# Fourth block's product added last, behind the next chunk's first three; down units at three places a chunk; forms made earlier

## The chip, the cores and the metric

One core of a Trainium2 chip runs the whole kernel in one launch. The metric is the device time of one execution in microseconds (us), the median of several runs; smaller is better. Engines are named as the profile names them: PE (TensorE matmuls), PEld (TensorE weight loads, which overlap PE), DVE (VectorE), ACT (ScalarE), POOL (GpSimd), SP (SyncE, which issues most transfers). L12 is line 12 of the kernel's file.

## The reference, cut to what matters

Two layers of an encoder trunk, for one sequence of 512 tokens and 1024 features, in float32:

```python
# a layer
h = rms_norm(x, attn_norm)
...                               # three branches: latent attention, grouped attention, pooling
x = x + merged @ w_out            # 1024 -> 1024, "out-projection"
# the feed-forward part (FFN)
h = rms_norm(x, ffn_norm)
ud = depthwise_conv(h @ w_up, w_conv, b_conv)    # 1024 -> 2 * 2816, conv of width 3 over tokens
gate, val = split(ud)
x = x + (silu(gate) * val) @ w_down              # 2816 -> 1024
```

The change touches the FFN, and the end of the out-projection where the FFN's inputs are made.

## The kernel before

**Layout.** Activations lie with features on the 128 partitions and the 512 tokens along the free axis. The residual is `XM`, eight rows (m = 0 to 7) of 128 features by 512 tokens. PE multiplies in a reduced float type, so every operand is held as two halves, high and low, whose sum is the float32 value; a product is three matmuls (high x high, high x low, low x high; `mm3`, L526). `HH` and `HL` are the halves of the scaled residual, `wh` and `wl` those of a weight, `ah` and `al` those of an activation. A low half is high subtracted from the value: on VectorE, on POOL, or "by transfer" (L438), where ScalarE writes the negated high half and a transfer that POOL issues adds the value onto it. All V., A. and G. calls pass through one-line wrappers, so the profile gives them few lines: L299 activation, L306 tensor_tensor, L310 scalar_tensor_tensor, L314 reduction, L318 tensor_scalar, L322 copy.

**The FFN's up-projection.** It has 22 chunks of 128 gate and 128 value features each. Chunks 0 to 3 are computed plainly: two units of 24 matmuls of 128x512 each (`plain`, tokens "u"). Chunks 4 to 21 are computed as 2x2 block products (gate and value by left and right halves of the features, against left and right 256 tokens), with seven products instead of eight (tokens "f", function `product`). Each product has a name, "11", "12", "1", "22", "2", "4", "3", and is twelve matmuls of 128x256, four for each pair of input rows q = 0 to 3 with three matmuls each. It needs one form of the weights (made by `w_form` from the chunk's four weight tiles a11, a12, a21, a22) and one form of the input (made once a layer by `build_forms(q)`). Forms 11, 12 and 22 of the weights are plain halves in tiles `fh` and `fl`, by transfer; forms 1, 2, 4 and 3 are sums or differences on VectorE (`total`), then halves in `wh` and `wl`.

For a chunk, 11 goes to PSUM bank acc; 2 and then 3 are added onto it. 1 goes to bank AV, and 4 is added onto it. 12 and 22 go to banks of their own with tag ST. Between them ScalarE copies intermediate values out to `sx` (keys s1, s5, s2, s4), and VectorE adds them into `u` (gate) and `v` (value): with product 3 done, VectorE does v[hi] = acc + s5, then v[lo] = acc + s4, where s4 is the copy of 22. Scaling, convolution, silu and the product of gate and value follow.

**The FFN's down-projection.** Tokens "d" are units of three matmuls of 128x512, for one output row m and one chunk. `_groups()` splits the 22 chunks in groups of 4, 5, 5, 5, 3; the units of a group become possible behind its last chunk, and are dealt over the chunks of the next group, at four places of a chunk: behind products 22, 2, 4 and 3 (SPOTS). Six units are kept for the end (KEEP times 3), and the last group's units stand behind the last chunk. Units of one m add up in one bank, tag mi or S in turn.

**What sets the order.** `_ffn()` writes a list of tokens, and PE follows it. The other engines' work is issued by a planner with costs in us (`chain`, whose argument `after` is how many us of planned PE time a chain waits before its steps are issued; `need(key)`, which issues what a key depends on before PE goes on; `free(tag)`, `slot(name)`). Weight forms are made six units ahead of PE (LAF), each weight tile is given back by `w_free`, and only then is the next tile's transfer issued. PSUM has eight banks: two acc, two ST, two AV, one mi, one S.

**At the end of the out-projection.** For each row m, 24 matmuls fill a bank, VectorE adds it to `XM[m]` (`resid`, L310), ScalarE makes `HH`, VectorE `HL` (L310), and the squares for the norm go through ScalarE and POOL (`sq`). Behind every second row `build_forms(q)` makes the input forms of rows 2q and 2q+1: two `hn` (scaled rows, L318), four differences `tt` (L306), then eight steps for the halves `tf`. Its chain is issued with after = 2.0 for q = 0 and 1, and 8.0 for q = 2 and 3. The first plain chunk follows on PE; its matmuls of row 7 need the last `HH` and `HL`.

Of the kernel before, what the change touches and what calls it, by code (L numbers as in the profile page):

```python
# [46 lines left out]
KEEP = 2  # L47
FORMS = ("11", "12", "1", "22", "2", "4", "3")
SPOTS = ("22", "2", "4", "3")
END = object()  # L50
# [62 lines left out]


def _ffn():

    toks, late = [], []
    for g, (c0, c1) in enumerate(_groups()):  # L120
        dealt = len(late) - (KEEP * SIZES[g - 1] if g == len(SIZES) - 1 else 0)
        for n, c in enumerate(range(c0, c1)):
            if g == 0:
                toks += [("u", c, 0), ("u", c, 1)]
                continue
            now = late[:dealt * (n + 1) // (c1 - c0) - dealt * n // (c1 - c0)]
            late = late[len(now):]
# [22 lines left out]
def _stream():  # L150


    pieces, slots, units, alone = [], [], [], []
    early, plain, fresh = [], 0, False
    for kind, *u in _layer_units() * L:
# [7 lines left out]
        if kind == "f":  # L163
            if u[1] == FORMS[0]:
                first, fresh = len(pieces), True
# [7 lines left out]
            units.append((u[1], first))  # L173
            continue
# [163 lines left out]
def trunk(ctx: ExitStack, tc: tile.TileContext, x, w, prm, gb, cst, out):  # L338
# [128 lines left out]
    def w_form(j, form, pi):  # L467
# [15 lines left out]
        dst, x, y, op, keys, gone = {  # L483
            "1": (a21, a21, a22, ALU.add, [], None),
            "2": (s2, a21, a11, ALU.subtract, [("sum", pi, "1")], 0),
            "4": (a12, a12, s2, ALU.subtract, [("sum", pi, "2")], None),
            "3": (s2, a22, s2, ALU.subtract, [("sum", pi, "4"), ("form", pi, "2")], 3)}[form]
# [195 lines left out]
    def layer(l, sq, xsrc):  # L683
# [904 lines left out]
        def build_forms(q):  # L1588
# [27 lines left out]
            chain(whole, sums, *[z for name in ("1", "2", "22", "3") for z in halves_of(name)], after=2.0 if q < 2 else 8.0)  # L1616

# [72 lines left out]

        quad = {}

        def product(c, name):

            if name == "11":
# [3 lines left out]
            if name in ("12", "1", "22"):  # L1699
                quad[name] = ps({"12": "ST", "1": "AV", "22": "ST"}[name])  # L1700
# [4 lines left out]
            if name == "3":  # L1705
                need(("s2", l, c))
            bank = quad[{"11": "a", "2": "a", "3": "a", "4": "1"}.get(name, name)]
            o = bank[:, 0:256]
            wh, wl = wnext()
            for q in range(4):  # L1710
                need(("tf", l, name, q))
                ws, (dh, dl) = slice(q * P, q * P + P), forms[name, q]
                mm3(o, wh[:, ws], wl[:, ws], dh, dl, q == 0 and name in ("11", "12", "1", "22"),
                    q == 3, name not in ("12", "22"))
            u, v, (sa, sb) = quad["u"], quad["v"], quad["s"]
# [17 lines left out]
            def scale(t):  # L1733
                return [([("rbc", G2)], lambda: V.tensor_tensor(t[:, :T], t[:, :T], fin["rbc"][:, :T], ALU.mult))]

            if name == "11":
                aside(sa[:, lo], "s1")
            elif name == "12":
                chain(([("s1", l, c)], add(u[:, lo], sa[:, lo], "ST")))
            elif name == "1":  # L1740
                aside(sb[:, lo], "s5")
            elif name == "22":
                aside(sb[:, hi], "s4", "ST")
            elif name == "2":
                aside(sa[:, hi], "s2")
            elif name == "4":
                chain(([("s2", l, c)], add(u[:, hi], sa[:, hi], "AV")), *scale(u), *convolve(c, 0, u))
            else:
                chain(([("s4", l, c)], add(v[:, hi], sb[:, lo])), add(v[:, lo], sb[:, hi], "acc"), *scale(v), *convolve(c, 1, v))

# [14 lines left out]
        def down(g, m, i):  # L1765
# [245 lines left out]
```

## Time and profile before

| | before |
|---|---|
| time, median of 3 runs | 1545.37 us (1545.33 to 1545.38) |
| span of the profiled execution | 1542.9 us (its own whole time is not listed; the median stands 2.5 above the span) |
| PE busy | 1536.2 us, 8337 matmuls |
| PEld busy | 1342.9 us |
| DVE busy | 1161.6 us, 1959 instructions |
| ACT busy | 1076.8 us, 2014 instructions |
| POOL busy | 766.8 us, 829 instructions |
| DMA | 243.36 MB, mean 158 GB/s |
| stretches with block products | 469 to 753 us and 1237 to 1521 us |

Rows of the timeline give the start of an instruction in us from the span's start, its duration in us, the engine, line, operation, output <- inputs, shape, and in brackets how long the engine had stood idle and what ended that. "x2" means that two neighbouring instructions of one kind are told in one row. Rows of waits give an engine and what it waited for, with the total, the number and the longest. The second layer repeats the first 767.8 us later.

### The profile page before, as it was taken

The page shows a single profiled execution, that of the slowest core. Times are in us where ns is not written, and L with a number is a line of the kernel's source. Part 1 is how long each engine was busy: PE and PEld are TensorE (multiplying, and loading weights), DVE is VectorE, ACT ScalarE, POOL GpSimd, SP SyncE. Part 2 cuts the span into 40 slices and gives each one's busy share as a digit, 9 for nine tenths or more (in the row PEclk, how much of TensorE's full clock was granted, in tenths as well). Part 3 has the DMA queues.
Part 4 walks back from the last instruction along what each step waited for, and adds up shares of the span by engine and source line. Part 5 has one row for each costly group of instructions (what it writes and reads, how often), then busy time and mean ns, then how long its engine had stood idle before and what let it go on. Part 6 is the DMA issues. An engine that isn't in the chain of part 4 may idle for free.

```text
span 1542.9 us, 24572 instructions
## 1 busy us (share of the span) xinstructions
PE 1536.2 (100%) x8337; PEld 1342.9 (87%) x8337; DVE 1161.6 (75%) x1959; ACT 1076.8 (70%) x2014; POOL 766.8 (50%) x829
## 2 busy tenths in 40 slices
PE   9999999999999999999999999999999999999999
PEld 8888888888889999999898888888888899999997
DVE  6777886776688888888746688768666888888885
ACT  6557875877677877777554587758766677777772
POOL 2884886753452323222588648766435522222222
PEclk9999999999999999999999999999999999999999
DMA  7432344658978878777454323547498778788763
GB/s 238 112 118 83 89 124 142 163 128 204 233 177 191 181 185 187 192 176 153 139 148 127 117 76 86 139 141 168 110 220 216 193 181 190 179 186 193 177 140 109
DMA packets 140381, 243.36 MB, mean 158 GB/s; under 512 B 31072, under 2 KB 53600, under 8 KB 140256
## 3 DMA queue, kind: packets, MB, share of 16 engines
q1 hardware_dynamic: 91872, 162.93, 33.9%
q0 software_dynamic: 43488, 78.66, 29.6%
q8 instruction: 65, 1.06, 0.3%
q10 hardware_dynamic: 4896, 0.21, 0.2%
q14 instruction: 60, 0.49, 0.1%
HBM read 149.41 MB, written 13.63 MB: 106 GB/s over the span
## 4 chain that ended last, share of the span: by engine, by line
PE 98%; DMA 1%; ACT 0%; DVE 0%; issue 0%; SPq 0%; POOL 0%; ACTq 0%; DVEq 0%
PE ps_acc L526 42%; PE ps_AV L526 19%; PE ps_ST L526 17%; PE ps_S L526 10%; PE ps_mi L526 10%; DMA qa<-nm 0%; DMA XM<-x 0%; DVE ka L322 0%; POOL wl L306 0%; ACT wh L299 0%; PE ps_mi L531 0%; PE ps_S L531 0%; SPq L407 0%; SPq L1835 0%; DVE XM L310 0%
## 5 line engine op out<-in xcount | busy, mean ns | idle before, releaser
L438 POOL DMA_DIRECT2D wl<-raw x194 | 175.5, 911 | 408.3 <-ACT wl L299 184.4
L299 ACT ACTIVATE wh<-raw 128x512 fp32r<-128x512 f32 (+2 forms) x449 | 265.0, 605 | 58.6 <-DVE raw L306 13.7
L306 POOL TENSOR_TENSOR wl<-raw,wh 128x512 fp32r<-128x512 f32 (+2 forms) x164 | 205.5, 1262 | 144.8 <-ACT wh L299 139.2
L438 POOL DMA_DIRECT2D fl<-raw x108 | 94.2, 873 | 168.2 <-ACT fl L299 66.2
L526 PE MATMUL ps_acc<-HH,wh 128*128 128x512 f32 x400 | 156.8, 392 | 0.4 <-DVE XM L310 0.4
L526 PE MATMUL ps_acc<-HH,wl 128*128 128x512 f32 x400 | 156.4, 391 | 0.0
L526 PE MATMUL ps_acc<-HL,wh 128*128 128x512 f32 x400 | 156.4, 391 | 0.0
L310 DVE SCALAR_TENSOR_TENSOR a<-u,prm,a 128x511 f32<-128x511 f32 x176 | 134.7, 768 | 18.7 <-ACT a L299 18.1
L299 ACT ACTIVATE wl<-wh 128x512 fp32r<-128x512 f32 (+1 forms) x194 | 121.9, 628 | 6.1
L314 DVE TENSOR_REDUCE nm<-ps_S 128x1 fp32r<-128x512 f32 x128 | 87.9, 687 | 44.5 <-PE ps_S L526 43.9
L299 ACT ACTIVATE a<-u,prm 128x512 f32<-128x512 f32 x88 | 71.2, 812 | 56.1 <-DVE u L306 56.0
L526 PE MATMUL ps_acc<-tf,wh 128*128 128x256 f32 x576 | 106.2, 282 | 0.0
L526 PEld LDWEIGHTS ps_acc<-tf,wh 128*128 128x128 f32 x576 | 94.3, 191 | 6.0
L526 PEld LDWEIGHTS ps_acc<-HH,wl 128*128 128x128 f32 x400 | 75.1, 188 | 16.3
L526 PEld LDWEIGHTS ps_acc<-HH,wh 128*128 128x128 f32 x400 | 75.4, 189 | 15.4 <-issue 0.7
L526 PEld LDWEIGHTS ps_acc<-HL,wh 128*128 128x128 f32 x400 | 75.2, 188 | 15.4
L526 PE MATMUL ps_acc<-tf,wl 128*128 128x256 f32 x288 | 81.5, 283 | 0.0
L526 PE MATMUL ps_AV<-HH,wl 128*128 128x256 f32 (+1 forms) x240 | 78.2, 326 | 0.0
L526 PE MATMUL ps_AV<-HH,wh 128*128 128x256 f32 (+1 forms) x240 | 78.2, 326 | 0.0
L526 PE MATMUL ps_AV<-HL,wh 128*128 128x256 f32 (+1 forms) x240 | 78.2, 326 | 0.0
L306 DVE TENSOR_TENSOR wl<-raw,wh 128x512 fp32r<-128x512 f32 (+1 forms) x92 | 64.3, 699 | 16.3 <-ACT wh L299 16.0
L306 DVE TENSOR_TENSOR pl<-ps_ST,ph 128x512 fp32r<-128x512 f32 x86 | 58.4, 683 | 18.5 <-ACT ph L299 15.0
(427 smaller groups left out, 5035.3 us busy)
## 6 DMA issues: line engine op xcount, KB each, us to landing
raw<-w SPq DMA_DIRECT2D x153, 512.0 KB, 4.0
wl<-raw POOLq DMA_DIRECT2D x190, 256.0 KB, 4.1
raw<-w SPq DMA_DIRECT2D x151, 256.0 KB, 3.8
fl<-raw POOLq DMA_DIRECT2D x108, 256.0 KB, 5.0
raw<-w SPq DMA_DIRECT2D x13, 384.0 KB, 3.1
XM<-x SPq DMA_DIRECT2D x16, 256.0 KB, 4.5
dtq<-tr SPq DMA_DIRECT2D x16, 192.0 KB, 2.1
dtk<-tr SPq DMA_DIRECT2D x16, 192.0 KB, 3.2
```

The source lines that it names most:

```text
L299: return self.eng.activation(out, in_, func, **k)
L306: return self.eng.tensor_tensor(out, *a)
L310: return self.eng.scalar_tensor_tensor(out, *a)
L314: return self.eng.tensor_reduce(out, in_, *a, **k)
L438: nc.gpsimd.dma_start(f(lo), r, accum_op=ALU.add)
L526: PE.matmul(o, lhsT=lhsT, rhs=rhs, start=start, stop=stop, skip_group_check=again)
```

## The change

In the FFN:

- FORMS is now 11, 1, 12, 22, 2, 4, 3, and the "22" token in a chunk's place is that of the chunk before: 11, 1 and 12 of chunk c, then 22 of chunk c - 1, then 2, 4 and 3 of chunk c. Chunk 4 has no 22 in that place, and chunk 21 has two, that of chunk 20 and its own.
- Except in chunk 21, product 22 has no bank of its own: it is added onto the chunk's acc bank, behind 11, 2 and 3. VectorE must first have read that bank for v[hi] (key `vh`); behind 22, ScalarE copies the bank to v[lo]. The copy to s4 and the VectorE addition for v[lo] are gone. Chunk 21 keeps the old way.
- Down units stand at three places of a chunk (behind 2, 4 and 3), and a group's units start 0, 1 or 2 places later (SKIP, `_dealt`). The bank of a down unit is chosen among mi and S by whichever is free soonest (also AV and ST, once no chunk is open).
- Weights: form 4's difference is computed together with form 3's total; the fourth tile (a22) is given back at form 22 instead of form 3.

Ahead of the FFN, `build_forms` has after = 2.0 for every q.

The numbers of instructions issued stay, but for 34 VectorE additions of 128x256 that are gone (17 a layer).

```diff
-FORMS = ("11", "12", "1", "22", "2", "4", "3")
-SPOTS = ("22", "2", "4", "3")
+FORMS = ("11", "1", "12", "22", "2", "4", "3")
+SPOTS = ("2", "4", "3")
+SKIP = (0, 1, 2, 2, 2)
...
+def _dealt():
+    starts = [len(SPOTS) * (c0 - SIZES[0]) + n for (c0, _), n in zip(_groups(), SKIP)]
+    at = [0] * (len(SPOTS) * (FC - SIZES[0]))
+    for g in range(1, len(SIZES)):
+        a, n = starts[g], starts[g + 1 if g + 1 < len(SIZES) else g] - starts[g]
+        units = KC * SIZES[g - 1]
+        if not n:
+            n = len(at) - a
+            units -= KEEP * SIZES[g - 1]
+        for s in range(n):
+            at[a + s] = units * (s + 1) // n - units * s // n
+    return at
...
             for f in FORMS:
-                toks.append(("f", c, f))
+                if f != "22" or c > SIZES[0]:
+                    toks.append(("f", c - (f == "22"), f))
+                if f == "22" and c == FC - 1:
+                    toks.append(("f", c, "22"))
                 if f in SPOTS:
-                    k = SPOTS.index(f)
-                    toks += now[len(now) * k // len(SPOTS):len(now) * (k + 1) // len(SPOTS)]
+                    k = next(dealt)
+                    toks += late[:k]
+                    late = late[k:]
...
             by_transfer(hi[:, :T], lo[:, :T], {"11": a11, "12": a12, "22": a22}[form])
             done("w", j)
+            if form == "22":
+                w_free(sl[3])
             return
...
         def total():
+            if form == "4":
+                return
+            if form == "3":
+                V.tensor_tensor(a12, a12, s2, ALU.subtract)
+                done("sum", pi, "4")
             V.tensor_tensor(dst, x, y, op)
             done("sum", pi, form)
-            if gone is not None:
-                w_free(sl[gone])
+            if form == "2":
+                w_free(sl[0])
...
-            chain(whole, sums, *[...], after=2.0 if q < 2 else 8.0)
+            chain(whole, sums, *[...], after=2.0)
...
+            if name == "22" and not ends:
+                need(("vh", l, c))
-            bank = quad[{"11": "a", "2": "a", "3": "a", "4": "1"}.get(name, name)]
+            bank = quad[{"11": "a", "2": "a", "3": "a", "4": "1", "22": name if ends else "a"}.get(name, name)]
...
+            elif name == "22" and ends:
+                aside(sb[:, hi], "s4", "ST")
             elif name == "22":
-                aside(sb[:, hi], "s4", "ST")
+                def low():
+                    A.activation(v[:, lo], o, AF.Copy)
+                    free("acc")
+                chain(low, *scale(v), *convolve(c, 1, v))
...
+            elif ends:
+                chain(([("s4", l, c)], add(v[:, hi], sb[:, lo])), add(v[:, lo], sb[:, hi], "acc"), *scale(v), *convolve(c, 1, v))
             else:
-                chain(([("s4", l, c)], add(v[:, hi], sb[:, lo])), add(v[:, lo], sb[:, hi], "acc"), *scale(v), *convolve(c, 1, v))
+                chain(([("s5", l, c)], add(v[:, hi], sb[:, lo])), lambda: done("vh", l, c))
...
-                state["tag"] = tags[m % 3] if ends else ("mi", "S")[m % 2]
+                state["tag"] = tags[m % 3] if ends else soonest("mi", "S", *(("AV", "ST") if not quads else ()))
```

The first place is VectorE at the end of layer 1's out-projection. `XM` from ps_acc is the residual of row 6, `XM` from ps_ST that of row 7, the last; the two `hn` and four `tt` are the forms of rows 4 and 5. Before:

```order
L310 SCALAR_TENSOR_TENSOR XM_83<-ps_acc_741_4609,XM_83 128x512
L310 SCALAR_TENSOR_TENSOR HL_85<-XM_83,prm0_91,HH_84 128x512
L310 SCALAR_TENSOR_TENSOR XM_83<-ps_ST_745_4665,XM_83 128x512
L310 SCALAR_TENSOR_TENSOR HL_85<-XM_83,prm0_91,HH_84 128x512
L318 TENSOR_SCALAR hn_746_4676<-XM_83,prm0_91 128x512
L318 TENSOR_SCALAR hn_747_4677<-XM_83,prm0_91 128x512
L306 TENSOR_TENSOR tt_748_4678<-hn_746_4676 128x256
L306 TENSOR_TENSOR tt_749_4679<-hn_747_4677,hn_746_4676 128x256
L306 TENSOR_TENSOR tt_748_4678<-hn_747_4677,tt_748_4678 128x256
L306 TENSOR_TENSOR tt_749_4679<-hn_747_4677,tt_748_4678 128x256
```

And now (17 lines further down in the file):

```order
L327 SCALAR_TENSOR_TENSOR XM_83<-ps_acc_741_4609,XM_83 128x512
L327 SCALAR_TENSOR_TENSOR HL_85<-XM_83,prm0_91,HH_84 128x512
L335 TENSOR_SCALAR hn_746_4676<-XM_83,prm0_91 128x512
L335 TENSOR_SCALAR hn_747_4677<-XM_83,prm0_91 128x512
L323 TENSOR_TENSOR tt_748_4678<-hn_746_4676 128x256
L323 TENSOR_TENSOR tt_749_4679<-hn_747_4677,hn_746_4676 128x256
L323 TENSOR_TENSOR tt_748_4678<-hn_747_4677,tt_748_4678 128x256
L323 TENSOR_TENSOR tt_749_4679<-hn_747_4677,tt_748_4678 128x256
L327 SCALAR_TENSOR_TENSOR XM_83<-ps_ST_745_4665,XM_83 128x512
L323 TENSOR_TENSOR tf_750_4680<-tt_748_4678,tf_750_4680 128x256
L327 SCALAR_TENSOR_TENSOR HL_85<-XM_83,prm0_91,HH_84 128x512
```

The six instructions for rows 4 and 5 moved ahead of the last residual, and one half `tf` ahead of the last `HL`. The second place is PE in chunk 5 of layer 1. Before, the end of the chunk's product 22 on a bank of its own (ps_ST), one down unit, and the start of product 2:

```order
L526 MATMUL ps_ST_841_5398<-tf_752_4682,fh_822_5265 128x256 x2
L526 MATMUL ps_ST_841_5398<-tf_752_4682,fl_823_5266 128x256
L526 MATMUL ps_ST_841_5398<-tf_765_4766,fh_822_5265 128x256 x2
L526 MATMUL ps_ST_841_5398<-tf_765_4766,fl_823_5266 128x256
L526 MATMUL ps_S_828_5316<-act01_4720,wh153_5189 128x512 x2
L526 MATMUL ps_S_828_5316<-act01_4720,wl153_5190 128x512
L526 MATMUL ps_acc_833_5331<-tf_723_4458,wh158_5288 128x256 x2
L526 MATMUL ps_acc_833_5331<-tf_723_4458,wl158_5289 128x256
```

And now, where ps_ST is the chunk's product 12, ps_acc_809 the acc bank of chunk 4 and ps_acc_828 that of chunk 5:

```order
L550 MATMUL ps_ST_831_5337<-HH_84,fl_816_5204 128x256
L550 MATMUL ps_acc_809_5140<-tf_724_4459,fh_817_5224 128x256 x2
L550 MATMUL ps_acc_809_5140<-tf_724_4459,fl_818_5225 128x256
L550 MATMUL ps_acc_809_5140<-tf_737_4569,fh_817_5224 128x256 x2
L550 MATMUL ps_acc_809_5140<-tf_737_4569,fl_818_5225 128x256
L550 MATMUL ps_acc_809_5140<-tf_752_4682,fh_817_5224 128x256 x2
L550 MATMUL ps_acc_809_5140<-tf_752_4682,fl_818_5225 128x256
L550 MATMUL ps_acc_809_5140<-tf_765_4774,fh_817_5224 128x256 x2
L550 MATMUL ps_acc_809_5140<-tf_765_4774,fl_818_5225 128x256
L550 MATMUL ps_acc_828_5297<-tf_723_4458,wh156_5244 128x256 x2
L550 MATMUL ps_acc_828_5297<-tf_723_4458,wl156_5245 128x256
```

The fourth product of the chunk is now 22 of the chunk before, on that chunk's acc bank, and no unit stands behind it.

More of the change, by code (lines that the diff above doesn't have):

```diff
@@ L153, in _stream @@
     pieces, slots, units, alone = [], [], [], []
-    early, plain, fresh = [], 0, False
+    early, plain, fresh, firsts = [], 0, False, {}
     for kind, *u in _layer_units() * L:
@@ L172, in _stream @@
                     alone.append(True)
-            units.append((u[1], first))
+            units.append((u[1], firsts[u[0]]))
             continue
@@ L1615, in build_forms @@
                 done("tf", l, name, q)
-            chain(whole, sums, *[z for name in ("1", "2", "22", "3") for z in halves_of(name)], after=2.0 if q < 2 else 8.0)
+            chain(whole, sums, *[z for name in ("1", "2", "22", "3") for z in halves_of(name)], after=2.0)
         for m in range(KC):
@@ L1698, in product @@
                 quad["a"] = ps("acc")
-            if name in ("12", "1", "22"):
+            ends = c == FC - 1
+            if name in ("12", "1") or name == "22" and ends:
                 quad[name] = ps({"12": "ST", "1": "AV", "22": "ST"}[name])
@@ L1712, in product @@
                 ws, (dh, dl) = slice(q * P, q * P + P), forms[name, q]
-                mm3(o, wh[:, ws], wl[:, ws], dh, dl, q == 0 and name in ("11", "12", "1", "22"),
-                    q == 3, name not in ("12", "22"))
+                mm3(o, wh[:, ws], wl[:, ws], dh, dl, q == 0 and (name in ("11", "12", "1") or name == "22" and ends),
+                    q == 3, name not in ("12", "22") or name == "22" and not ends)
             u, v, (sa, sb) = quad["u"], quad["v"], quad["s"]
```

22 lines of the change are left out of this document (11 added, 11 removed).

## The prediction

> **What bounds the kernel now.** The page comes first: the span, the busy times and the chain that ended last.
>
> ```profile
> span 1542.9 us, 24572 instructions
> PE 1536.2 (100%) x8337; PEld 1342.9 (87%) x8337; DVE 1161.6 (75%) x1959; ACT 1076.8 (70%) x2014; POOL 766.8 (50%) x829
> PE 98%; DMA 1%; ACT 0%; DVE 0%; issue 0%; SPq 0%; POOL 0%; ACTq 0%; DVEq 0%
> ```
>
> PE is busy for 1536.2 of 1542.9 us and makes 98% of the chain, so a change is worth what it does to PE's sequence: fewer matmuls, a shorter pitch, or fewer waits. Next come PE's own waits, the longest three of five rows (the other two are 0.2 each), and then the two stretches in which the changed loop runs (the chunks in 2x2 blocks, once a layer).
>
> ```profile
> PE ps_ST L526 <- DMA qa<-nm: 1.5, 1, 1.5
> PE ps_mi L1832 <- DVE keep L334: 1.1, 1, 1.1
> PE ps_acc L526 <- DVE XM L310: 0.4, 1, 0.4
> ...
> 469.00:753.00 284.00, 284.00 (x1960) 265.08 (x1959) 232.90 (x391) 212.76 (x396) 80.68 (x91) 1.00 0.77 175
> 1237.00:1521.00 284.00, 284.00 (x1959) 264.92 (x1959) 232.73 (x390) 212.57 (x395) 80.71 (x91) 1.00 0.77 174
> ```
>
> The columns of the last two are sum, then busy us (and count) of PE, PEld, DVE, ACT, POOL, then granted clock, DMA share, GB/s. In both stretches PE never stands idle at a clock of 1.00. But a matmul's end is modelled, so short waits hide inside busy time; the starts show them. Six rows of PE's timeline in the first stretch, two from the run of units behind the last chunk, and four around the one place where starts jump:
>
> ```profile
> 491.09 0.63 PE L526 MATMUL ps_S<-act,wh 128*128 128x512 f32 x2
> 491.79 0.62 PE L526 MATMUL ps_mi<-act,wh 128*128 128x512 f32 x2
> 492.48 0.28 PE L526 MATMUL ps_AV<-HH,wh 128*128 128x256 f32 x1
> 493.91 0.63 PE L526 MATMUL ps_mi<-act,wh 128*128 128x512 f32 x2
> ...
> 753.10 0.39 PE L526 MATMUL ps_S<-ah,wh 128*128 128x512 f32 x1
> 753.77 0.39 PE L526 MATMUL ps_S<-ah,wh 128*128 128x512 f32 x1
> ...
> 1295.92 0.28 PE L526 MATMUL ps_ST<-HL,fh 128*128 128x256 f32 x1
> 1296.16 0.39 PE L526 MATMUL ps_ST<-HH,fl 128*128 128x256 f32 x1
> 1296.38 0.28 PE L526 MATMUL ps_ST<-HH,fh 128*128 128x256 f32 x1
> 1296.50 0.28 PE L526 MATMUL ps_ST<-HL,fh 128*128 128x256 f32 x1
> ```
>
> A 256-wide matmul starts 0.12 us behind the one before (1296.38 to 1296.50), so a product of twelve takes 1.44. A down unit (three of 512) takes 0.67 to 0.68 inside a long run (753.10 to 753.77), but 0.70 and 0.69 as first and second unit behind a product (491.09, 491.79, 492.48); the product behind them takes 1.43 (to 493.91). So a run of two units costs about 0.70 + 0.69 - 2 x 0.68 - 0.01 = 0.02 us for the change of width and back. At 1296.16 and 1296.38 PE started 0.12 and 0.10 late: it waited for a form's transfer, 0.2 in all.
>
> How much could any order gain here? A stretch holds 18 chunks x 7 products x 12 = 1512 matmuls of 256 and 1960 - 1512 = 448 of 512: 1512 x 0.12 + 448 x 0.227 = 283.1 of 284.0 us. Both layers together have under 2 us to give.
>
> **The change, part by part.**
>
> *The matmuls.* Their number and shapes stay: the seventh product moves, and adds onto the bank where it stood alone. That is 0 on PE.
>
> *Evacuations.* ScalarE's copy of the fourth block's product to sx becomes its copy to the result, one for one. VectorE loses one 128x256 addition for each chunk but the last.
>
> ```profile
> L306 DVE TENSOR_TENSOR u<-ps_acc,sx 128x256 f32<-128x256 f32 x36 | 14.8, 418 | 0.0
> ```
>
> 17 x 2 x 0.418 = 14 us less on VectorE, which is not on the path: 0.
>
> *Runs of down units.* By the order there are 72 runs of units a layer before, and 53 now (three places in a chunk instead of four). Of the old ones 8 are single units, which cost PE less. 71 runs behind which a product follows become 52: some 19 x 2 fewer at 0.02, less for the single ones: **-0.5 us** (bounds -0.3 and -0.8 by the rounding of the rows).
>
> *Forms sooner, in this loop.* Form 1 is made ahead of 12, the difference for form 4 together with that for 3, and the fourth tile is given back only behind the form of 22, so it is held through the next chunk's first three. The late transfer at 1296.16 was that of 12; it now has one product more before it, and I take **-0.2**. The transfers stay as many:
>
> ```profile
> fl<-raw POOLq DMA_DIRECT2D x108, 256.0 KB, 5.0
> ```
>
> Each lands 5.0 us (median) behind its issue, and forms are made six units ahead, over 8 us of PE work at 1.44 and 0.68. So the cover is PE's own products; bounds 0 and the 0.2 a time seen above, taken 0.
>
> *The new wait.* Product 22 adds onto a bank that VectorE must first have read (`vh`). How soon that read ends shows before:
>
> ```profile
> 481.83 0.63 PE L526 MATMUL ps_S<-act,wh 128*128 128x512 f32 x2
> 482.90 0.42 DVE L306 TENSOR_TENSOR u<-ps_acc,sx 128x256 f32<-128x256 f32 x1
> ```
>
> Product 3 of that chunk ended at 481.83 and the read at 483.32, 1.5 us later. Now two down units and three products stand between, 2 x 0.68 + 3 x 1.44 = 5.7 us: 0, with 4 us in hand. What is queued behind it on PE is the whole loop, so if that cover were gone every chunk would pay. Units behind a group start a place or two later, so they wait for less: 0.
>
> *Forms of the input, two groups of which start 2 us behind their residual instead of 8.* Here something moves onto the path. On VectorE the scaling and differences for rows 4 and 5 (two hn, four tt) now stand ahead of the last residual (XM from ps_ST) and its low half (HL); before, they stood behind both. First those rows as they ran, then an earlier group of the same shape, then POOL, ScalarE and PE:
>
> ```profile
> 423.68 0.75 DVE L310 SCALAR_TENSOR_TENSOR HL<-XM,prm,HH 128x512 fp32r<-128x512 f32 x1 [0.79 <-ACT HH L299]
> 425.44 0.69 DVE L310 SCALAR_TENSOR_TENSOR XM<-ps_ST,XM 128x512 f32<-128x512 f32 x1 [1.00 <-PE ps_ST L526]
> 426.92 0.96 DVE L310 SCALAR_TENSOR_TENSOR HL<-XM,prm,HH 128x512 fp32r<-128x512 f32 x1 [0.79 <-ACT HH L299]
> 427.80 3.70 DVE L318 TENSOR_SCALAR hn<-XM,prm 128x512 f32<-128x512 f32 x2
> ...
> 412.61 0.88 DVE L318 TENSOR_SCALAR hn<-XM,prm 128x512 f32<-128x512 f32 x2
> 413.40 0.42 DVE L306 TENSOR_TENSOR tt<-hn 128x256 f32<-128x256 f32 x1
> 414.07 2.42 DVE L306 TENSOR_TENSOR tt<-hn,tt 128x256 f32<-128x256 f32 x2
> 419.54 2.75 DVE L306 TENSOR_TENSOR tf<-tt,tf 128x256 fp32r<-128x256 f32 x2 [0.40 <-ACT tf L299]
> ...
> 419.29 1.28 POOL L306 TENSOR_TENSOR wl<-raw,wh 128x512 fp32r<-128x512 f32 x1 [2.25 <-ACT wh L299]
> 420.55 1.46 POOL L306 TENSOR_TENSOR sq<-sq,sqt 128x512 f32<-128x512 f32 x1
> 424.78 1.29 POOL L306 TENSOR_TENSOR wl<-raw,wh 128x512 fp32r<-128x512 f32 x1 [1.95 <-ACT wh L299]
> 426.05 1.28 POOL L306 TENSOR_TENSOR sq<-sq,sqt 128x512 f32<-128x512 f32 x1
> 427.89 1.59 POOL L306 TENSOR_TENSOR sq<-sq,sqt 128x512 f32<-128x512 f32 x1
> 429.14 1.57 POOL L306 TENSOR_TENSOR wl<-raw,wh 128x512 fp32r<-128x512 f32 x1
> ...
> 426.16 0.72 ACT L299 ACTIVATE HH<-XM,prm 128x512 fp32r<-128x512 f32 x1 [0.28 <-DVE XM L310]
> ...
> 430.00 0.39 PE L526 MATMUL ps_acc<-HH,wh 128*128 128x512 f32 x1
> 430.22 0.39 PE L526 MATMUL ps_acc<-HL,wh 128*128 128x512 f32 x1
> ```
>
> PE needs the last HL at 430.22; it was there at 427.88, 2.34 early. From the start of the residual to the end of HL it took 427.88 - 425.44 = 2.44 (ScalarE's HH lies between). VectorE is free at 424.43, so now hn starts about 424.4. Undisturbed, two hn and four tt take some 2.26 (hn 0.40 apart by 412.61 and 413.40, tt 0.33 to 0.46): residual at 426.6, HL at 429.1, still 1.1 early. That is the lower bound, 0.
>
> But POOL runs two operations back to back from 424.78 to 427.33, and such pairs hold VectorE up. At 427.80 an hn, 0.4 long elsewhere, lasted until both POOL operations from 427.89 were over (the two hn 3.70 against 0.88); at 419.54 two tf took 2.75 instead of 0.75, one POOL operation each. The nearest row is 427.80: same instruction, same two POOL operations, 0.09 apart. By it the second hn (about 424.76, against POOL's 424.78) ends some 3.1 us behind 424.78, at 427.9; four tt follow, the residual starts at 429.3 and HL ends at 431.7: PE waits 1.5. By 419.54 and 420.55 the two operations are paid by two instructions and two to three tt remain: residual at 428.4 to 428.9, HL at 430.9 to 431.3, PE waits 0.7 to 1.1. I take 1.1, between the rows, with ends 0 and 1.5; both layers stand alike, so **+2.2** (0 to +3.0).
>
> The Trainium skill, page "SBUF — State Buffer", section "Who interferes with whom", has a rule for this: VectorE's second port pair is GpSimd's, a lock that an instruction with two SBUF inputs, or in a two-port mode, takes against a GpSimd operation that reads SBUF; whoever issues first holds it for the whole instruction and the other fully blocks. That these pairs exclude each other, the trace agrees; that the first to issue goes first it does not, since the hn at 427.80 began 0.09 ahead of POOL and ended last. By the rule the second hn would go first here, and the wait would be the smaller one, 0.7.
>
> Behind it, the forms of rows 6 and 7 now stand ahead of the norm's constant (fac), on which a POOL operation of 3.10 us and the transfers queued behind it on POOL wait:
>
> ```profile
> 436.03 3.10 POOL L306 TENSOR_TENSOR fac<-fac,mhalf 128x16 f32<-128x16 f32 x1 [4.44 <-DVE fac L318]
> ```
>
> That may start up to 2 us later, but PE is then about 1.1 later too: between 0 and 0.5, taken 0.
>
> **Sum.** -0.5 - 0.2 + 2.2 = +1.5 us. The page's execution has a span of 1542.9; its own whole time is not listed, and the runs' median of 1545.37 stands 2.5 above the span. Both move alike: 1545.37 + 1.5 = **1546.9**. About 0.2% (3.1 us) is what a measurement of this kernel tells from no change, so this is no change.
>
> **Rivals.** (1) No blocking: POOL's pair falls elsewhere, the last residual stays in time, and only the -0.7 is left: 1544.7. For it: 1.1 us of slack undisturbed. Against: POOL's two operations depend on ScalarE's rows, which the change leaves ahead of it. Chance 0.18. (2) The first to issue goes first: 0.7 a layer, -0.7 + 1.4, so 1546.1; chance 0.22 (the page's rule, against the row at 427.80). (3) Slower: product 22, or the forms behind the tile held longer, waits in every chunk. The place is PE's fourth product of a chunk; from 3.1 / 34 = 0.09 us a chunk it decides, and at 0.15 it is +5 us, so 1551 with half the rest. For it: VectorE is busy 232.90 of 284, and one form came late already. Against: 4 us in hand at the new wait and a longer lead for the forms. Chance 0.13. (4) Layer 2's attention: the 1.5 us wait for qa<-nm, which layer 1 does not have, goes with the shift, 1545.4, or finds a second one, 1548.4; chance 0.07.
>
> **Numbers.** The forecast (0.7 to 1.5 a layer) has 0.40. Its own range is 1546.1 to 1547.7. The range of all reaches from no blocking with part of the qa<-nm wait gone, 1544.0, to the forecast's upper end with a further wait of that size, 1549.0; outside it lie most of rival 3 and a little below. Faster by over 0.2% would need 3.1 us where the loop holds under 2 and the waits 1.5: 0.02. Slower by over 0.2%: rival 3 and a part of 4, 0.16. The rest, 0.82, is within.
>
> **What would show it.** Right: PE's row for the last HL of the first plain chunk starts 0.7 to 1.5 us behind the matmul before it, in both layers, with the last XM on VectorE at 428.4 or later and a stretched hn or tt before it. In the loop, three runs of units a chunk, and no jump in starts at the fourth product. The addition from ps_acc falls from 36 to 19 a stretch. Wrong: jumps of 0.1 us or more at each fourth product (rival 3); the last residual at 426.6 (rival 1); a long wait in layer 2's attention at another place.

## The result, and the profile after

The changed kernel took 1549.97 us (median of 5 runs, 1548.80 to 1552.71), the kernel before in the same comparison 1545.33 (1543.10 to 1545.38): a ratio of 1.0040, 95% interval 1.0029 to 1.0051. It is slower by 4.6 us, outside the predicted range of 1544.0 to 1549.0. The profiled execution of after has a span of 1547.0 (its own whole time: 1548.8), 4.1 over the 1542.9 of before; the account below is for that pair.

The head of the page of after:

```profile
span 1547.0 us, 24499 instructions
PE 1538.3 (99%) x8337; PEld 1343.1 (87%) x8337; DVE 1154.5 (75%) x1925; ACT 1082.7 (70%) x2014; POOL 769.4 (50%) x829
```

PE's waits in after that before did not have (us in total, times, longest):

```profile
PE ps_ST L550 <- DMA wl<-raw: 3.3, 3, 1.7
...
PE ps_acc L550 <- DVE HL L327: 0.3, 1, 0.3
PE ps_acc L550 <- ACT sx L316: 0.2, 1, 0.2
```

PE is still the bound, with the same number of matmuls. New are waits for transfers of low halves of weights. Where the time went is read from starts of the same matmuls in PE's timeline (first column): row 0 of the out-projection with `mgh`, the first product of chunk 4, the first norm of layer 2, and the first two again in layer 2. Before:

```profile
381.71 0.39 PE L526 MATMUL ps_acc<-mgh,wh 128*128 128x512 f32 x1
469.00 0.28 PE L526 MATMUL ps_acc<-HH,fh 128*128 128x256 f32 x1
788.82 0.29 PE L526 MATMUL ps_S<-prt,C 128*128 128x16 f32 x2
1149.53 0.39 PE L526 MATMUL ps_acc<-mgh,wh 128*128 128x512 f32 x1
1236.82 0.28 PE L526 MATMUL ps_acc<-HH,fh 128*128 128x256 f32 x1
```

After:

```profile
381.60 0.39 PE L550 MATMUL ps_acc<-mgh,wh 128*128 128x512 f32 x1
472.33 0.28 PE L550 MATMUL ps_acc<-HH,fh 128*128 128x256 f32 x1
792.41 0.29 PE L550 MATMUL ps_S<-prt,C 128*128 128x16 f32 x2
1151.40 0.39 PE L550 MATMUL ps_acc<-mgh,wh 128*128 128x512 f32 x1
1240.70 0.28 PE L550 MATMUL ps_acc<-HH,fh 128*128 128x256 f32 x1
```

| from, to | before | after | difference |
|---|---|---|---|
| start of the span to the first row | 381.71 | 381.60 | -0.1 |
| rest of out-projection and plain chunks, layer 1 | 87.29 | 90.73 | **+3.4** |
| loop with block products and last units, layer 1 | 319.82 | 320.08 | +0.3 |
| layer 2 up to the same row | 360.71 | 358.99 | -1.7 |
| rest of out-projection and plain chunks, layer 2 | 87.29 | 89.30 | **+2.0** |
| loop to the end of the span, layer 2 | 306.08 | 306.30 | +0.2 |

So the loop that the change rewrites is level, and its way in costs 5.4 us. Most of the -1.7 is the one wait for qa<-nm of before (1.5), which this execution does not have.

**The last residual.** VectorE, POOL and PE at the end of layer 1's out-projection, after:

```profile
425.03 1.52 DVE L323 TENSOR_TENSOR tt<-hn 128x256 f32<-128x256 f32 x1
426.47 1.51 DVE L323 TENSOR_TENSOR tt<-hn,hn 128x256 f32<-128x256 f32 x1
...
428.69 0.68 DVE L327 SCALAR_TENSOR_TENSOR XM<-ps_ST,XM 128x512 f32<-128x512 f32 x1
...
430.16 0.75 DVE L327 SCALAR_TENSOR_TENSOR HL<-XM,prm,HH 128x512 fp32r<-128x512 f32 x1 [0.46 <-ACT HH L316]
...
424.67 1.60 POOL L323 TENSOR_TENSOR wl<-raw,wh 128x512 fp32r<-128x512 f32 x1 [1.93 <-ACT wh L316]
426.23 1.46 POOL L323 TENSOR_TENSOR sq<-sq,sqt 128x512 f32<-128x512 f32 x1
...
430.18 0.49 PE L550 MATMUL ps_acc<-HH,wh 128*128 128x512 f32 x1
430.97 0.50 PE L550 MATMUL ps_acc<-HL,wh 128*128 128x512 f32 x1 [0.29 <-DVE HL L327]
```

Two tt last 1.5 instead of 0.42, each until one POOL operation is over; the residual starts at 428.69, and HL ends at 430.91. PE's losses here and below are read from its starts: a start is late by what it comes more than the usual pitch (0.227 behind a matmul of 512, 0.12 behind one of 256) after the one before. PE loses 0.97 here in layer 1, and nothing in layer 2.

**Behind the norm.** The constant fac in after, and rbc made from it (fac in the shape of a row of tokens, by which VectorE multiplies every sum of a plain chunk as it takes it out of its bank, u<-ps,rbc); then ScalarE, POOL and PE at the last plain weight (act<-a there writes the high half of a chunk's result):

```profile
438.10 3.04 POOL L323 TENSOR_TENSOR fac<-fac,mhalf 128x16 f32<-128x16 f32 x1 [3.54 <-DVE fac L335]
...
442.56 0.70 DVE L347 STREAM_TRANSPOSE rbc<-fac 128x512 f32<-128x512 f32 x1
...
457.81 0.63 ACT L316 ACTIVATE act<-a 128x512 fp32r<-128x512 f32 x1 [2.33 <-DVE a L323]
...
459.51 0.63 ACT L316 ACTIVATE wl<-wh 128x512 fp32r<-128x512 f32 x1
...
460.56 0.88 POOL L455 DMA_DIRECT2D wl<-raw  x1 [0.22 <-issue]
...
465.15 0.39 PE L550 MATMUL ps_ST<-HL,wh 128*128 128x512 f32 x1
467.20 0.50 PE L550 MATMUL ps_ST<-HH,wl 128*128 128x512 f32 x1 [1.66 <-DMA wl<-raw]
```

The same copy and transfer before:

```profile
454.50 0.63 ACT L299 ACTIVATE wl<-wh 128x512 fp32r<-128x512 f32 x1
...
455.66 0.88 POOL L438 DMA_DIRECT2D wl<-raw  x1
```

On POOL fac began 0.57 behind the start of the norm's second matmul before (that at 435.46), and 2.44 behind it now (435.67), since VectorE has two hn, four tt and a tf ahead of it (2.19 in layer 2). That matmul itself stands three matmuls of 512 (0.68) sooner in PE's order than before: 151 instead of 148 matmuls lie between it and chunk 4's first product. So against the plain matmuls fac is 1.2 later in layer 1 and 0.9 in layer 2. The copies of the last plain weight now stand on ScalarE behind act<-a, which waits 2.33 for VectorE; they run 5 us later than before, the transfer is issued at 460.56 instead of 455.66, and PE, which needed it at 465.4, starts at 467.20. Of these 5 us, rbc accounts for 1.8 (it is ready 7.59 behind the norm's matmul instead of 5.80); the rest goes with the new order of the steps ahead of them. The transfer's landing took longer too (6.6 against 3.3). Summed over all starts from the norm's matmul on for 60 us, PE is late by 2.65 in layer 1 (0.45 at 448.9, 1.93 at 467.2, 0.27 in chunk 4) and by 2.39 in layer 2. Before, it is 0.00.

### The profile page after: what moved, and what is told of

Same layout as the page of the kernel before. It is cut to its first block, busy times and chain, and to the rows that moved or that the text cites. A ratio compares the mean times of both kernels' runs of the same rounds, so it can differ in the third digit from the quotient of the medians.

```text
span 1547.0 us, 24499 instructions
## 1 busy us (share of the span) xinstructions
PE 1538.3 (99%) x8337; PEld 1343.1 (87%) x8337; DVE 1154.5 (75%) x1925; ACT 1082.7 (70%) x2014; POOL 769.4 (50%) x829
## 4 chain that ended last, share of the span: by engine, by line
PE 91%; DVE 3%; issue 2%; ACT 2%; POOL 2%; DMA 1%; POOLq 0%; ACTq 0%; DVEq 0%
PE ps_acc L550 42%; PE ps_AV L550 17%; PE ps_ST L550 12%; PE ps_mi L550 10%; PE ps_S L550 9%; POOL wl L323 1%; DVE a L327 1%; ACT a L316 0%; DMA wl<-raw 0%; POOL wl L455 0%; ACT wh L316 0%; DVE tt L323 0%; DVE XM L327 0%; DVE tf L323 0%; POOL sq L323 0%
## 5 line engine op out<-in xcount | busy, mean ns | idle before, releaser
L323 DVE TENSOR_TENSOR u<-u,rbc 128x512 f32<-128x512 f32 x72 | 49.7, 690 | 31.0 <-ACT u L316 30.2
```

What stands on the lines that cost most here:

```text
L323: return self.eng.tensor_tensor(out, *a)
```

## The experiments

A sum "behind the norm" below is that sum of late starts, for layer 1 and layer 2, in the one execution that was profiled. Times are medians, ratios go to the kernel before in the same comparison.

### Which part of the change costs it

```diff
- chain(whole, sums, ..., after=2.0)                       # changed kernel
+ chain(whole, sums, ..., after=2.0 if q < 2 else 8.0)     # x1: as before
```

> The changed kernel with one edit undone: build_forms has after = 2.0 for q = 0 and 1 and 8.0 for q = 2 and 3 again; the loop stays as changed. Theory A (the early input forms alone cost the time: in the changed kernel's first layer PE waits 0.97 us for the last XM and HL, 0.45 and 1.93 us for low halves of plain weights, 0.27 us in chunk 4): these waits go, the fewer runs of units stay (-0.5) and the late transfer of form 12 stays gone (-0.2), so 1544.6, 5 us under the changed kernel. Theory B (the loop's order costs it, since the weights' forms and transfers were reordered and reach back into the plain chunks): the wait for a weight's low half near 465 us stays and the time is 1548.5 to 1550.

Measured 1543.55, ratio 0.9996 (0.9987 to 1.0005), no wait behind the norm (0.00, 0.00) and none at the last HL. The other way round, the kernel before with after = 2.0 for every q:

> The kernel before with one edit: build_forms has after = 2.0 for every q. Theory A: the same waits as in the changed kernel at the end of the out-projection and in the plain chunks, without the gain in the loop: 1550, with a wait near 465 us of 1.5 to 2 us and one for HL near 430 us of 0.5 to 1. Theory B: only the wait for HL, 0.5 to 1 in the first layer, so 1546.

Measured 1552.68, ratio 1.0054 (1.0041 to 1.0066), sums 2.50 and 3.33. Its longest waits lie at another place than expected (chunk 4's product 22, not 465 us). So theory A stands: that one argument costs all of it, and the loop's new order costs nothing. In the old loop the argument costs more (8.4 against the kernel before; 6.0 in the new loop, x7 below against x1): there PE loses 1.1 and 1.2 at the last HL, in both layers. With q = 2 late alone (after = 8.0) and with q = 3 late alone:

> The changed kernel, but the forms of rows 4 and 5 (q = 2) late again (after = 8.0), those of rows 6 and 7 (q = 3) early. Theory A1 (the wait for HL comes from q = 2, the late low halves from q = 3, whose forms stand ahead of the norm's constant, so that POOL's fac, rbc and all activation steps behind them are late, and ScalarE's weight copies behind those): the wait near 430 us is gone, that near 465 us stays: 1549. Theory A2 (the late low halves come from q = 2, by the delay of the residual that it causes): both waits are gone: 1545.

> The changed kernel, but the forms of rows 6 and 7 (q = 3) late again (after = 8.0), those of rows 4 and 5 (q = 2) early. Theory A1: the wait for HL near 430 us stays (0.5 to 1), that near 465 us is gone: 1545.5. Theory A2: both stay: 1549 to 1550.

Measured 1546.76 (1.0016, 1.0007 to 1.0025) and 1547.30 (1.0020, 1.0011 to 1.0029). Neither A1 nor A2 holds: the wait at 465 is gone in both, but a wait for chunk 4's copy to sx on ScalarE comes in its place (2.0 and 0.5 for x3, 0.7 and 0.7 for x4). The wait for the last HL is gone in x3 and stays in x4 (0.46 by the starts, in layer 1 alone), as both theories said. Either early group alone costs some 3 us. In x4, fac is not late:

```profile
436.82 2.93 POOL L323 TENSOR_TENSOR fac<-fac,mhalf 128x16 f32<-128x16 f32 x1 [1.71 <-DVE fac L335]
...
440.97 1.16 POOL L455 DMA_DIRECT2D wl<-raw  x1
```

It begins 0.56 behind the norm's matmul (436.26), the transfer behind it is issued 4.71 behind it (4.90 before), and rbc is ready 6.41 behind it (5.80 before, but the matmul stands 0.68 sooner in PE's order here too). On VectorE the two hn of rows 6 and 7 now stand ahead of rbc and their four tt between rbc and the first sums. So early forms can make PE wait in chunk 4 with fac in time; how x4's waits come about was not followed further.

### The order on ScalarE

```diff
- chain(([("rbc", G2)], scale), *convolve(c, part, u))
+ chain(([("rbc", G2)], scale), *convolve(c, part, u), after=2.0)
```

> The changed kernel with one number added: the chain of a plain chunk (scaling, convolution, silu, product) has after = 2.0 instead of 0.2. On ScalarE the copies wh143 and wl143 of the last plain weights then stand ahead of the copy act<-a of chunk 1 instead of behind it; the input forms stay early. Theory C (head of the line: the weight's low half is late because its copies stand on ScalarE behind an activation step that waits for VectorE): the waits near 465 us (1.9) and in the second layer near 1234 (1.7) are gone, those for HL stay, so 3 to 3.6 us under the changed kernel's 1549.97: 1546.5. Theory D (the transfer is late because the constant fac and with it rbc come 2 us later, or because the queue is slow, whatever ScalarE's order): a wait of over 1 us stays near 465 us, and the time stays within 1 us of 1549.97.

Measured 1549.67, ratio 1.0035 (1.0022 to 1.0047). The copies ran at 455.41 to 457.20, and the waits at 465 and 1234 are gone, as theory C says. The time is not: PE now waits 0.4 at 449 and 0.8 for sx in chunk 4, and 1.7 at 1218 in layer 2 (sums 1.75 and 1.99). So the order on ScalarE has a part in where PE pays.

The changed kernel a second time:

> The changed kernel itself, once more. If the waits at the loop's entry are what it pays, a second profile has them at the same places with sizes within 0.5 us; the spread of its times (1548.8 to 1552.7) is then that of these waits and of layer 2's attention. If they are an accident of the first profile, other places show.

Measured 1549.52 (1548.74 to 1551.36); sums 2.62 and 2.44, with layer 2's wait at 1217 (1.67) where the first profile had it at 1234 (1.64). The size repeats, the place does not.

### The late constant

In the late-forms kernel (x1), a power of 128x10 into an unused tile ahead of fac on POOL; and in the changed kernel, the power of fac itself taken away:

```diff
+ nc.gpsimd.tensor_tensor(junk, a[:, :10], bc(mhalf, [P, 10]), ALU.pow)          # x9, ahead of fac
...
- G.tensor_tensor(a, a, bc(mhalf, [P, 16]), ALU.pow)                             # x10, FFN norms
+ nc.gpsimd.tensor_tensor(a, a, bc(mhalf, [P, 16]), ALU.mult)
```

> The kernel with late input forms (q = 2 and 3 at 8.0) and the changed loop, with one POOL operation more in each layer: a power of 128x10 into an unused tile stands right ahead of the norm's constant fac of the FFN, at no cost in the plan, so that every order stays. It makes rbc about 1.9 us later, as in the changed kernel (7.6 us behind the norm's matmul instead of 5.8). Theory G (the late constant alone makes PE wait, since every evacuation and activation of the plain chunks hangs on rbc and the weights' copies stand among them on ScalarE): 1.5 to 2.5 us of waits a layer come, at plain weights' low halves or chunk 4's sx, so 3 to 5 us over the kernel without it. Theory H (what counts is the order of ScalarE and VectorE that the early forms bring about): no waits over 0.3 us, no change of time.

> The changed kernel, with the power on POOL in the FFN's two norms replaced by a multiplication (the root is left out; the plan counts the power's cost, so every order stays). It takes some 2.7 us less than 3.04, so rbc is ready some 5 us behind the norm's matmul, sooner than before the change (5.8). Theory G: the waits behind the norm's matmul (2.6 in the first layer, 2.4 in the second) go, those for the last XM and HL stay: 1545. Theory H: they stay within 1 us of what they were: 1548.5 to 1549.5.

Measured 1550.05 (1.0034, 1.0021 to 1.0048) with sums 1.82 and 4.88 for x9, and 1544.87 (1.0001, 0.9992 to 1.0010) with sums 0.00 and 0.00 for x10. POOL's row in x10:

```profile
439.12 0.31 POOL L666 TENSOR_TENSOR fac<-fac,mhalf 128x16 f32<-128x16 f32 x1 [3.54 <-DVE fac L335]
```

With every order of the changed kernel kept, a fac that takes 0.31 instead of 3.04 removes all waits behind the norm; with every order of x1 kept, a fac 2.2 to 2.5 later makes such waits. So the changed kernel's waits hang on when fac is done, theory G. That its delay alone makes them is not shown: in x10 rbc is ready 3.93 behind the norm's matmul, sooner than before the change (5.80), and x9's delay is about twice that of the changed kernel against PE's plain matmuls. The order has a share: in x10, though rbc is so early, the copies of the last plain weight still run 1.1 later against the plain matmuls than before. And x9's waits stood at the transfers right behind fac in POOL's queue, which were late too: it did not tell rbc from the queue. x13 and x14 do, in x1's order; x15 and x16, which leave the root out, in the changed kernel's:

```diff
+ for _ in range(3): nc.vector.transpose(rbc..., ...)              # x13: rbc later
+ nc.gpsimd.tensor_tensor(junk, a[:, :10], ..., ALU.pow)           # x14: behind fac, POOL's queue later
...
+ subtract instead of pow, and 6 more transposes                   # x15: queue sooner, rbc late
+ subtract instead of pow, and pow of 128x13 behind it             # x16: rbc sooner, queue late
```

> The kernel with late input forms (q = 2 and 3 at 8.0) and the changed loop; in each layer's FFN norm VectorE writes rbc four times instead of once (0.63 apart, outside the plan, so every order stays). rbc is then ready 1.9 us later, but POOL's queue behind fac (a low half and a transfer) runs on time. Theory G1 (the constant rbc is what counts: evacuations and activations hang on it, and weights' copies stand among those on ScalarE): waits of 1.5 us or more a layer, at a low half near 465 us or at chunk 4's sx, 3 us or more in time. Theory G2 (POOL's queue behind fac is what counts): no waits over 0.5 us, no change.

> The same kernel, but with a power of 128x10 into an unused tile right behind fac on POOL (2.15 us in an earlier run), outside the plan: rbc on time, POOL's low half and the transfer behind it some 1.9 us later. Theory G1: at most 0.5 us of waits a layer. Theory G2: a wait for a plain weight's transfer near 448 us and 1216 us of 1.5 us or more each, 3 us or more in time.

> The changed kernel with early input forms and all its orders; in the FFN's norms POOL's power is replaced by a subtraction (the root left out), so that POOL's queue behind fac runs 2.7 us sooner than in the changed kernel, and VectorE writes rbc seven times instead of once, so that rbc is ready about as late as there (7.6 to 8.5 us behind the norm's matmul). Theory G1' (in the changed kernel's order, where the copies of the last plain weight stand on ScalarE behind act<-a, the late rbc makes the waits near 465 and 1234 us, POOL's queue those near 448 and 1217): a wait of 1 us or more near 465 us or at chunk 4's sx in each layer, 1547 or more. Theory G2 (POOL's queue alone): only the waits for the last XM and HL: 1545.

> The changed kernel likewise, but with rbc soon and POOL's queue late: the subtraction instead of the power, and a power of 128x13 into an unused tile behind it on POOL. rbc is ready some 4 us behind the norm's matmul, the low half and the transfers behind fac are about where they are in the changed kernel. Theory G1': the waits near 465 and 1234 us are gone, a wait of 0.3 to 2 us near 448 and 1217 us stays. Theory G2: all waits of the changed kernel stay, 2.4 us or more a layer, 1549 to 1550.

| | time | ratio (95%) | profiled execution | behind the norm |
|---|---|---|---|---|
| x13: x1's order, rbc 2.2 later | 1543.38 | 0.9993 (0.9984 to 1.0002) | 1543.39 | 0.1, 0.1 |
| x14: x1's order, POOL's queue 2.0 to 2.6 later | 1548.60 | 1.0028 (1.0017 to 1.0039) | 1552.44, the longest of 8 | 3.68, 4.82 |
| x15: changed order, rbc late, queue sooner | 1553.08 | 1.0057 (1.0045 to 1.0070) | 1554.39 | 4.67, 4.75 |
| x16: changed order, rbc soon, queue late | 1547.61 | 1.0020 (1.0012 to 1.0029) | 1545.16, the shortest of 12 | 0.53, 0.25 |

(In x14 and x15, and in x9's second layer, some 1.6 us of a sum is a lower clock behind the wait, see the last section.) PE's waits for weights, for x14, then x15, then x16 (x13 has none):

```profile
PE ps_ST L550 <- DMA wl<-raw: 4.9, 2, 3.0
```

```profile
PE ps_ST L550 <- DMA wl<-raw: 4.4, 2, 2.2
...
PE ps_AV L550 <- DMA wl<-raw: 0.8, 2, 0.4
```

```profile
PE ps_ST L550 <- DMA wl<-raw: 0.3, 1, 0.3
```

Two paths hang on fac. With the late forms' order only POOL's queue matters (G2): x13's rbc is harmless, since the last plain weight's copies stand ahead of act<-a on ScalarE. With the changed order rbc matters most (G1'): it holds act<-a, and the copies wait behind it. The sizes are not those of the changed kernel: against PE's plain matmuls its rbc and its queue are 1.1 later than before, where x9, x13 and x14 add 2.0 to 2.6 and x15 has rbc 1.9 late; only x16's queue is as late (1.0). So the runs show which path pays in which order, and not how the 2.65 and 2.39 divide. x16's median lies 2.7 over x10's, though its profile (a span of 1543.4) shows under 1 us of waits behind the norm; where its other executions lose the rest was not profiled.

### VectorE and POOL at the last residual

x6 gives chunk 0's value weights their low halves by transfer, x11 leaves out POOL's addition of row 6's squares.

> The changed kernel, but the weights of chunk 0's value half (two units) get their low halves by transfer too, so that the two POOL additions wl<-raw,wh near 419 and 425 us are gone (POOL issues two transfers instead, ScalarE makes two more copies). VectorE's order to the last HL stays but for one tf. Theory E (VectorE's tt are held by POOL's additions one for one): only one of the two tt is stretched, by sq, so the last residual starts 1.1 to 1.3 us sooner, near 427.5, and the wait for HL near 430 us in the first layer (0.97) is gone or under 0.2; the late low halves stay in part, so 1547.5 to 1549. Rival F (VectorE was held by something else, the queue order on ScalarE or the transfers on SBUF): the residual stays at 428.4 or later, and the wait at 0.5 or more.

> The changed kernel, without POOL's addition of row 6's squares (left out of the FFN's norm; orders stay). It is the second of the two POOL operations that ran beside VectorE's four tt in the first layer. If POOL's operation is what held the second tt (1.51 us against 0.41), that tt takes 0.4 to 0.5, the last residual starts near 427.6 instead of 428.69, and PE's wait for the last XM and HL in the first layer (0.97) falls below 0.2. If it was something else, the tt stays above 1 us. Theory G adds that the waits behind the norm's matmul stay (2.4 to 2.6), since fac comes as late behind that matmul, so the time falls by 1 us at most: 1548.6.

x6: 1549.22 (1.0028, 1.0019 to 1.0037). E's time for the residual missed, and by the numbers rival F's came: it started at 430.00 and PE lost 1.50. POOL's wl addition was gone, but sq came later (428.17) and held the last of the tt for 1.97, and the row before had come late as well. x11: 1549.34 (1.0030, 1.0019 to 1.0041). VectorE there:

```profile
425.47 1.52 DVE L323 TENSOR_TENSOR tt<-hn 128x256 f32<-128x256 f32 x1
426.91 0.41 DVE L323 TENSOR_TENSOR tt<-hn,hn 128x256 f32<-128x256 f32 x1
...
428.03 0.69 DVE L327 SCALAR_TENSOR_TENSOR XM<-ps_ST,XM 128x512 f32<-128x512 f32 x1
```

The tt beside the removed operation falls from 1.51 to 0.41, the other keeps its 1.52, and PE's 0.97 at the last HL is gone. So one POOL operation held one tt. Behind the norm 2.46 and 2.38 stay, and the median hardly moves (1549.34 against x7's 1549.52).

### The loop's own gain

x1 with four places for the units instead of three:

```diff
- SPOTS = ("2", "4", "3")
+ SPOTS = ("22", "2", "4", "3")
```

> The changed kernel with the input forms late for q = 2 and 3, and the down units at four places of a chunk again (behind 22, 2, 4 and 3). One look, for the starts of matmuls in the two stretches of the loop. If a run of units costs 0.018 us by its change of width, some 19 more runs bring 0.3 us a layer back, and no new waits stand; the span is 0.6 us over that of the kernel with three places, less than a look at the time can tell.

> The loop as changed but with units at four places of a chunk, and the input forms late for q = 2 and 3, now timed: by its one look it has neither the waits at the loop's entry nor those of 0.27 us a layer in the last group, so it is level with the kernel with three places and the late forms, and with the kernel before: 1543.5 to 1544.3.

x8, a single execution, had a span of 1542.2; x12 measured 1543.71, ratio 0.9997 (0.9989 to 1.0006). By the starts the stretches of 284 us take 0.22 and 0.24 longer with four places than with three (single waits apart). But with three, the units behind the last chunk start some 0.25 late in each layer, in a wait for VectorE, which makes the last chunk's act; with four they do not. From the first product of chunk 4 to layer 2's norm it is 319.77 with four, 319.98 with three (x1), 319.82 before. Neither x1 nor x12 is told from the kernel before, so no version here beats it.

## Why the prediction was wrong

- **The step that failed**: "Behind it, the forms of rows 6 and 7 now stand ahead of the norm's constant (fac) [...] That may start up to 2 us later, but PE is then about 1.1 later too: between 0 and 0.5, taken 0." Both delays were about as put: in layer 1 fac began 2.1 later in the span (438.10 against 436.03), and PE's plain matmuls behind it came 0.9 later. Wrong was the price of the difference, 2.65 and 2.39 us instead of 0 to 0.5. What hung on fac had little in hand; the first transfer behind it on POOL and the matmul that uses it, before and after:

```profile
440.36 0.88 POOL L438 DMA_DIRECT2D wl<-raw  x1
...
447.69 0.39 PE L526 MATMUL ps_ST<-HH,wl 128*128 128x512 f32 x1
```

```profile
442.36 0.89 POOL L455 DMA_DIRECT2D wl<-raw  x1
...
448.92 0.50 PE L550 MATMUL ps_ST<-HH,wl 128*128 128x512 f32 x1 [0.18 <-DMA wl<-raw]
```

Before, that transfer landed at 447.16, 0.5 ahead of its use; now at 448.88, and PE is 0.45 late. That slack was there to be read, for each transfer of the plain chunks, and was not.
- **ScalarE was left out of the move.** This is the larger part in layer 1 (1.93 here, 1.65 in x7). The sentence looked at POOL's queue alone. On ScalarE the last plain weight's copies went behind act<-a, and the slack at 465 was gone: before, that transfer landed at 458.99, 5 us ahead of its use.
- **The last residual**: forecast 1.1 a layer, measured 0.97 and 0. The mechanism (two tt, one POOL operation each; residual at 428.4 to 428.9) is what the first layer shows. In the second, VectorE went first, the residual came in time, and the term was 0.
- **Runs of units**: 0.26 a layer less by the starts, as forecast (-0.5). It was given back in the last group, where the sum had no term.
- **The late form of product 12** (-0.2): the wait at 1296 is gone; a like one of 0.22 stands at 1461 in x1, so nothing is shown.
- **Rivals.** No wait at any fourth product: rival 3's mechanism did not come, though its side of the outcome did. Rival 4's wait for qa<-nm went from this profile, but x2 with the same early forms has it (1.3): it comes and goes with the execution.
- The range's upper end held nothing for fac, although the text itself named a delay of 2 us; with 2 us a layer the sum itself would have been 1550.9.
- **Luck.** In the profiled pair the waits at the last HL and behind the norm come to 6.0 us, while the span grew by 4.1: the wait for qa<-nm of before happened to be missing. That, and a last residual cheaper than forecast, made the miss look smaller than the failed step is (5.0 us where 0 stood).

## What to carry to other kernels

When work is moved ahead of a small operation, list everything that hangs on that operation's result and on its engine's queue, and read for each the time between its landing and its use; the smallest is the delay that the move may bring before PE pays. Where orders are fixed in advance, a copy that stands behind a step of another chain inherits that chain's delay, so look at each engine's new order and not only at the engine on which the work was moved. In x5 the fix of one such wait moved it to the next places; what took all waits behind the norm away was the move undone (x1), or fac made early (x10, which leaves the root out).

## What the runs showed of the hardware

**The same pair went two ways.** In both profiles of the changed kernel, POOL's addition began 0.43 behind the first hn in layer 1 and in layer 2. In layer 1 the tt were held, 1.5 each. In layer 2 the first tt went ahead, POOL's addition was held (2.59 instead of 1.28), and of the tt only the last two were longer than elsewhere (1.85 together instead of 0.87):

```profile
1194.82 0.42 DVE L323 TENSOR_TENSOR tt<-hn 128x256 f32<-128x256 f32 x1
1195.16 0.42 DVE L323 TENSOR_TENSOR tt<-hn,hn 128x256 f32<-128x256 f32 x1
1195.49 1.85 DVE L323 TENSOR_TENSOR tt<-hn,tt 128x256 f32<-128x256 f32 x2
...
1194.46 2.59 POOL L323 TENSOR_TENSOR wl<-raw,wh 128x512 fp32r<-128x512 f32 x1 [1.95 <-ACT wh L316]
```

What decides it can't be seen from the starts: in both layers POOL's addition began ahead of the first tt. The rule of the Trainium skill, page "SBUF — State Buffer", section "Who interferes with whom", that who issues first holds the pair, therefore fits layer 1 and not layer 2, though that the two exclude each other shows again.

**Behind gaps of 2.24 us and more between starts, PE ran at a lower clock.** In x15 PE's start at 469.26 came 2.54 behind the one before; matmuls of 512 then started 0.43 apart instead of 0.227, for some 3 us:

```profile
469.77 0.63 PE L550 MATMUL ps_ST<-HH,wh 128*128 128x512 f32 x1
470.19 0.63 PE L550 MATMUL ps_ST<-HL,wh 128*128 128x512 f32 x1
```

The stretch from 470 to 474 us, columns as in the windows above (sum, busy of PE, PEld, DVE, ACT, POOL, granted clock, DMA share, GB/s):

```profile
470.00:474.00 4.00, 4.00 (x13) 3.12 (x13) 2.99 (x6) 1.97 (x4) 0.00 (x0) 0.65 0.97 235
```

The granted clock of that stretch is 0.65, and some 1.6 us are lost besides the wait. The same stretched starts stand behind gaps between starts of 2.24 (x14), 2.30 (x3) and 3.4 (x9); behind 2.17 (x6), 2.12 (x5) and the 2.05 of the changed kernel they do not. The Trainium skill, page "TensorE: Matmul & The Clock Gate", part 1, gives half clock after an idle window of about 3.4 us; here a shorter gap was enough.
